# Mixing products over pairs of units, one of them on GpSimd, with transposes six units ahead

## The chip, the cores and the metric

The kernel runs on one core of a Trainium2 chip. The metric is the device time of one execution in microseconds (us); lower is better. Engines are named as the profile has them: PE is TensorE, DVE VectorE, ACT ScalarE, POOL GpSimd, SP SyncE (which only issues transfers here).

## The reference

Token mixing of an RWKV block over x of 16 batches × 2048 positions × 256 features, in float32:

```python
x_prev[:, 1:, :] = x[:, :-1, :]           # the position before; zeros at the start
...
xv = x * time_mix_v + x_prev * (1 - time_mix_v)
xr = x * time_mix_r + x_prev * (1 - time_mix_r)
...
v = xv @ value_weight
r = xr @ receptance_weight
...
out = (1 / (1 + exp(-r)) * v) @ output_weight
```

k of the reference is not used by its output. The kernel leaves it out.

## The kernel before, in words

**Units.** A batch has 2048 positions, and position p·16 + j lies in partition p, block j. A unit is four blocks of one batch, 512 positions; there are four units a batch and 64 in all. For each unit the kernel transposes x (features into partitions), mixes, projects twice (r and v), gates, projects to the output, and stores.

**The mix.** The weights are scaled by the mixing coefficient t at the start (`w_bf`), so what remains is x + c·x_prev with c = 1/t − 1 (`c_sb`). Transposed x of a batch lies in one tile `xt` with 17 slots of 128 columns: slot 1 + j holds block j, and slot 0 is block 15 moved on by one partition, a *wrap copy* (`wrap_slots`, L324), since the position before block 0 of a partition is block 15 of the partition before. x_prev of columns lo to hi is then `xt[lo:hi]` and x is `xt[lo+128:hi+128]`. So a mix is a *product*, c times `xt[lo:hi]`, one for each half `ko` of the 256 features, 128x512 each (on VectorE in `scale`, L206; on GpSimd in `scale_pool`, L216; on ScalarE in `scale_act`, L371, in the last units), and a *sum* of both halves at once, 128x1024 (`add`, L228). A *piece* is one unit's mix m: m = 0 for r, m = 1 for v.

**One iteration of the loop, unit g.** TensorE: `psum_r` (4 matmuls, L239), the transposes of a later unit (8, `ps_t`, L172), `psum_v` (4, L239), the output matmuls of unit g − 1 (8, `psum_o`, L249). ScalarE: the sigmoid `s_sb` (L390), the copy of the transposes to `xt` (L177), the copy of the output to `o_sb` (L269). VectorE: products and sums of later units, then z = s_sb · psum_v (L412), then one more sum that is *held* until behind z. GpSimd: its products, and the issue of the loads of x (L90, which also cast to bfloat16). SyncE: the stores (L259).

**What sets the order.** Each engine runs its instructions in the order in which the loop writes them; semaphores join the engines. `advance` writes the transposes of all units up to a limit: `START_T[g]` at first, then g + `LOOK`, four units ahead. It also issues the load of batch b + 2 when unit 1 of batch b is transposed. From iteration `AHEAD` (8) on, an iteration works on piece 1 of unit g + 1 and piece 0 of unit g + 2: VectorE makes the product of half 0 of both and the sum of the first; GpSimd makes the products of half 1 of both pieces of unit g + 2; the sum of piece 0 of unit g + 2 is held behind z. A manual dependency lets GpSimd start only after the last sum ahead of z.

**Buffers.** `psum_r`, `psum_v` and `psum_o` have one buffer each, `ps_t` two, `xt`, `x_bf` and `o_sb` three (a batch each), `mix` two (a batch each). So psum_v of unit g + 1 can't start before z of unit g has read its own.

Of the kernel before, what the change touches and what calls it, by code (L numbers as in the profile page):

```python
# [15 lines left out]
def kernel(  # L16
# [26 lines left out]
    KO = D // P  # L43
    J = S // P
    UJ = 4
    TU = UJ * P
    UB = J // UJ
    NU = B * UB
    LOOK = 4
    H = UJ // 2  # L50
    START_T = [1, 3, 5, 6, 7]
    AHEAD = 8
    WARM = 34
    WARM2 = 12

# [14 lines left out]
    late_copies = []  # L70
# [132 lines left out]
    def scale(piece, kos=(0, 1)):  # L203
        b, m, lo, hi = piece
        for ko in kos:
            nc.vector.tensor_scalar(  # L206
                out=mix[b][:, m, ko, lo:hi],
                in0=xt[b][:, ko, lo:hi],
                scalar1=c_sb[:, m, ko : ko + 1],
                scalar2=None,  # L210
                op0=ALU.mult,
            )

    def scale_pool(piece, after):
        b, m, lo, hi = piece
        op = nc.gpsimd.tensor_scalar(  # L216
            out=mix[b][:, m, 1, lo:hi],
            in0=xt[b][:, 1, lo:hi],
            scalar1=c_sb[:, m, 1:2],
            scalar2=1.0,  # L220
            op0=ALU.mult,
            op1=ALU.mult,
        )
        tc.add_manual_dep(op.ins, after.ins.name, SYNC, reason="one at a time")

    def add(piece):
        b, m, lo, hi = piece
        return nc.vector.tensor_tensor(  # L228
            out=mix[b][:, m, :, lo:hi],
            in0=mix[b][:, m, :, lo:hi],  # L230
            in1=xt[b][:, :, lo + P : hi + P],
            op=ALU.add,
        )

    def project(ps, g, m, lo=0, hi=TU):
        b, e = divmod(g, UB)
        for mo in range(KO):
            for ko in range(KO):
                nc.tensor.matmul(  # L239
                    out=ps[:, mo, :],  # L240
                    lhsT=w_bf[:, m, ko, mo * P : (mo + 1) * P],
                    rhs=mix[b][:, m, ko, e * TU + lo : e * TU + hi],
                    start=(ko == 0),
                    stop=(ko == KO - 1),
                )
# [15 lines left out]
    def output(g, z):  # L261
        b, e = divmod(g, UB)
        if e == 0:
            o_sb[b] = opool.tile([P, J, D], FP32, name="o_sb")
        ps = ps_o_pool.tile([P, UJ, D], FP32, name="psum_o")
        for jj in range(UJ):
            out_matmuls(ps, z, jj, jj)
        j0 = e * UJ
        nc.scalar.copy(out=o_sb[b][:, j0 : j0 + UJ, :], in_=ps)  # L269
        if b == B - 1:  # L270
            store(nc.sync, b, j0, j0 + UJ)
        elif e % 2 == 1:
            store(nc.sync, b, j0 - UJ, j0 + UJ)
# [31 lines left out]
    def tile_for(b):  # L305
        if b not in mix:
            mix[b] = mixpool.tile([P, 2, KO, J * P], BF16, name="mix")

    def pieces(g):

        b, e = divmod(g, UB)
        tile_for(b)
        return [(b, m, e * TU, (e + 1) * TU) for m in range(2)]

    def ready(g):

        b, e = divmod(g, UB)
        return tnext > (g if b == 0 else UB * b + min(e + 1, UB - 1))

    def wrap_slots():  # L320
        while late_copies:
            b = late_copies.pop()
            if b > 0:
                nc.vector.tensor_copy(  # L324
                    out=xt[b][:, :, 1:P], in_=xt[b][:, :, J * P : (J + 1) * P - 1]
                )

    tnext = 1

    def advance(limit):  # L330
        nonlocal tnext
        while tnext <= min(limit, NU - 1):
            b, e = divmod(tnext, UB)
            if e == 1 and 2 < b + 2 < B:
                load(b + 2)
            transposes(tnext)
            tnext += 1
# [23 lines left out]
    scale(pieces(1)[0])  # L361
    add(pieces(1)[0])

    z_prev = None
    elsewhere = set()
    done = 3

    def scale_act(piece, kos):
        b, m, lo, hi = piece
        for ko in kos:  # L370
            nc.scalar.activation(  # L371
                out=mix[b][:, m, ko, lo:hi],
                in_=xt[b][:, ko, lo:hi],
                func=ACT.Copy,
                scale=c_sb[:, m, ko : ko + 1],
            )
            elsewhere.add((piece, ko))

    for g in range(NU - 1):


        lead = 2 * g + (4 if g < AHEAD else 5)
        todo = [pieces(k // 2)[k % 2] for k in range(done, min(lead, 2 * NU))]
        held = todo[-1:] if lead <= 2 * NU else []
        done = lead

        ps_r = ps_r_pool.tile([P, KO, TU], FP32, name="psum_r")
        project(ps_r, g, 0)
        s_sb = zpool.tile([P, KO, TU], BF16, name="s_sb")
        nc.scalar.activation(out=s_sb, in_=ps_r, func=ACT.Sigmoid)  # L390
        advance(START_T[g] if g < len(START_T) else g + LOOK)
        if g + LOOK >= NU and g + 2 < NU:
            scale_act(pieces(g + 2)[1], (0,))
        by_pool = []
        if 0 < g < NU - 2 and ready(g + 2):
            by_pool = [p for p in pieces(g + 2) if p not in todo or p in held]
        elsewhere.update((p, 1) for p in by_pool)
        for p in todo:
            if p[0] in late_copies:
                wrap_slots()  # L400
            if g > 0:
                scale(p, [ko for ko in range(KO) if (p, ko) not in elsewhere])
        for p in todo:
            if p not in held:
                last = add(p)
        ps_v = ps_v_pool.tile([P, KO, TU], FP32, name="psum_v")
        project(ps_v, g, 1)
        if g == 0:
            scale_act(todo[0], (0, 1))
            advance(2)  # L410
        z_sb = zpool.tile([P, KO, TU], BF16, name="z_sb")
        nc.vector.tensor_tensor(out=z_sb, in0=s_sb, in1=ps_v, op=ALU.mult)  # L412
        for p in by_pool:
            if p[0] in late_copies:
                wrap_slots()
            scale_pool(p, last)
        for p in held:
            add(p)
        if z_prev is not None:
            output(g - 1, z_prev)  # L420
        z_prev = z_sb
# [31 lines left out]
```

## Time and profile before

| | before |
|---|---|
| median of 3 runs | 226.84 us (226.77 to 227.25) |
| profiled execution, its own time | 226.7 us |
| its span, first to last instruction | 224.9 us |
| mean granted clock of TensorE | 0.997 |
| HBM read, written | 34.47 MB, 33.55 MB (302 GB/s over the span) |
| VectorE products of 512 (L206), mean | 356 ns, 128 of them |
| GpSimd products of 512 (L216), mean | 694 ns, 122 of them |
| ScalarE idle ahead of the output copy (L269) | 26.6 us in all |

Durations overlap by some tens of ns on VectorE, since an instruction is counted until its last write while the next has begun; the distance from start to start is what an instruction costs there. A matmul's row lasts longer than its share of TensorE for the same reason. "Idle before" is the engine's rest ahead of an instruction, with what ended it.

### The profile page before, as it was taken

The numbers are of one execution on the slowest core, as the hardware profiler recorded it, in microseconds if no ns is written. First come the engines' busy times: TensorE is split into PE (matmuls) and PEld (weight loads), VectorE is DVE, ScalarE is ACT, GpSimd is POOL, SyncE is SP. The second block draws the span as 40 slices with busy tenths as digits, with TensorE's granted clock in tenths as the row PEclk, the third lists the DMA queues.
The fourth block names the chain that finished last, engine by engine and source line by source line (L and its number), as shares of the span: only waits on it lengthen the run. The fifth ranks groups of instructions, "written<-read, shape, count | busy, mean of one in ns | idle before, by whom it ended". The sixth has DMA issues, their size and how long they took to land.

```text
span 224.9 us, 4329 instructions
## 1 busy us (share of the span) xinstructions
PE 211.0 (94%) x1593; PEld 136.4 (61%) x1593; DVE 211.8 (94%) x354; ACT 186.5 (83%) x202; POOL 96.0 (43%) x165
## 2 busy tenths in 40 slices
PE   8799898999999999999999999999999999999891
PEld 7556564666666566666656665665666566665570
DVE  1899999999999999999999999999999999999982
ACT  2699799789888888988888898788889888888771
POOL 1714525435435452543445254344525443443420
PEclk9999999999999999999999999999999999999998
DMA  6999999696988969697896969789696974444255
GB/s 191 190 198 222 240 283 318 254 200 249 255 251 249 248 258 191 258 249 238 256 252 251 200 262 230 235 256 259 240 203 258 236 233 197 187 188 189 114 230 217
DMA packets 9341, 51.92 MB, mean 231 GB/s; under 512 B 996, under 2 KB 1896, under 8 KB 3688
## 3 DMA queue, kind: packets, MB, share of 16 engines
q0 software_dynamic: 3008, 16.39, 40.3%
q1 hardware_dynamic: 6016, 34.87, 39.1%
q10 hardware_dynamic: 296, 0.40, 0.5%
q8 instruction: 12, 0.20, 0.3%
q14 instruction: 9, 0.07, 0.1%
HBM read 34.47 MB, written 33.55 MB: 302 GB/s over the span
## 4 chain that ended last, share of the span: by engine, by line
DVE 79%; issue 6%; PE 6%; DMA 3%; POOL 1%; SPq 1%; DVEq 0%; ACT 0%; POOLq 0%
DVE mix L228 40%; DVE z_sb L412 29%; DVE mix L206 9%; DMA x_unit<-in_x_dram 3%; PE psum_v L239 2%; POOL mix L216 1%; PE psum_o L249 1%; DVE xt L324 1%; PE psum_r L239 1%; PE ps_t L172 1%; PE psum_o L172 0%; ACT xt L177 0%; PE ps_t L239 0%; DVEq L412 0%; SPq L102 0%
## 5 line engine op out<-in xcount | busy, mean ns | idle before, releaser
L216 POOL TENSOR_SCALAR mix<-xt,c_sb 128x512 bf16<-128x512 bf16 x122 | 83.4, 694 | 112.6 <-DVE mix L228 101.8
L228 DVE TENSOR_TENSOR mix<-mix,xt 128x1024 bf16<-128x1024 bf16 (+1 forms) x129 | 105.2, 817 | 0.3 <-DVE mix L206 0.2
L269 ACT COPY o_sb<-psum_o 128x1024 f32<-128x1024 f32 x62 | 62.8, 1013 | 26.6 <-PE psum_o L249 26.6
L239 PEld LDWEIGHTS <-w_bf 128*128 128x128 bf16 x520 | 49.7, 97 | 45.9 <-issue 7.2
L412 DVE TENSOR_TENSOR z_sb<-s_sb,psum_v 128x1024 bf16<-128x1024 bf16 x63 | 76.2, 1209 | 0.6 <-PE psum_v L239 0.4
L239 PE MATMUL psum_v<-mix,w_bf 128*128 128x512 bf16 (+1 forms) x256 | 65.1, 376 | 5.9 <-DVE z_sb L412 4.6
L239 PE MATMUL psum_r<-mix,w_bf 128*128 128x512 bf16 (+1 forms) x256 | 65.3, 377 | 0.2
L390 ACT ACTIVATE s_sb<-psum_r 128x1024 bf16<-128x1024 f32 x63 | 65.0, 1031 | 0.2
L249 PE MATMUL psum_o<-wo_bf,z_sb 128*128 128x256 bf16 x500 | 64.9, 273 | 0.0
L177 ACT COPY xt<-ps_t 128x1024 bf16<-128x1024 bf16 x62 | 63.1, 1021 | 0.0
L249 PEld LDWEIGHTS <-z_sb 128*128 128x128 bf16 x512 | 50.0, 98 | 19.2
L206 DVE TENSOR_SCALAR mix<-xt,c_sb 128x512 bf16<-128x512 bf16 (+1 forms) x132 | 42.6, 355 | 2.0 <-ACT xt L177 0.5
L172 PEld LDWEIGHTS <-x_bf 128*128 128x128 bf16 x496 | 32.6, 98 | 15.1 <-DMA x_bf<-in_x_dram 1.4
L172 PE MATMUL ps_t<-ident,x_bf 128*128 128x128 bf16 x496 | 37.5, 219 | 0.4 <-DMA x_bf<-in_x_dram 0.3
L90 POOL DMA_DIRECT2D x_bf<-in_x_dram x19 | 11.0, 582 | 0.3 <-issue 0.3
L128 PE MATMUL ps_t<-zeros 128*128 128x128 bf16 x46 | 4.6, 289 | 1.0 <-DVE zeros L78 1.0
L128 PEld LDWEIGHTS <-zeros 128*128 128x128 bf16 x46 | 4.3, 135 | 1.0 <-DVE zeros L78 1.0
L146 DVE COPY tm<-psum_o 128x4 f32<-128x4 f32 x1 | 0.2, 161 | 3.5 <-PE psum_o L142 3.5
L324 DVE COPY xt<-xt 128x254 bf16<-128x254 bf16 x15 | 3.2, 213 | 0.0
L111 ACT ACT_TABLE_LOAD x1 | 1.3, 1283 | 2.0 <-issue 2.0
L371 ACT ACTIVATE mix<-xt,c_sb 128x512 bf16<-128x512 bf16 x4 | 2.8, 722 | 0.0
L172 PE MATMUL psum_o<-ident_f,x_unit 128*128 128x128 f32 x8 | 1.1, 276 | 1.6 <-DMA x_unit<-in_x_dram 1.6
(45 smaller groups left out, 21.5 us busy)
## 6 DMA issues: line engine op xcount, KB each, us to landing
out_dram<-o_sb SPq DMA_DIRECT2D x30, 1024.0 KB, 5.1
x_bf<-in_x_dram POOLq DMA_DIRECT2D x14, 1024.0 KB, 11.8
x_bf<-in_x_dram POOLq DMA_DIRECT2D x4, 256.0 KB, 6.2
out_dram<-o_sb SPq DMA_DIRECT2D x2, 512.0 KB, 2.6
out_dram<-o_sb SPq DMA_DIRECT2D x3, 256.0 KB, 2.1
x_unit<-in_x_dram SPq DMA_DIRECT2D x2, 256.0 KB, 3.6
x_unit<-in_x_dram SPq DMA_DIRECT2D x1, 512.0 KB, 6.5
x_bf<-in_x_dram POOLq DMA_DIRECT2D x1, 512.0 KB, 8.9
```

The source lines that it names most:

```text
L90: nc.gpsimd.dma_start(out=x_bf[b][:, lo:hi, :], in_=rows(b)[:, lo:hi, :])
L128: nc.tensor.matmul(out=ps, lhsT=zeros, rhs=zeros, start=True, stop=True)
L172: nc.tensor.transpose(out=ps[:, ko, jj * P : (jj + 1) * P], in_=src[:, jj, ko * P : (ko + 1) * P], identity=idn,)
L177: nc.scalar.copy(out=xt[b][:, :, c0 : c0 + TU], in_=ps)
L206: nc.vector.tensor_scalar(out=mix[b][:, m, ko, lo:hi], in0=xt[b][:, ko, lo:hi], scalar1=c_sb[:, m, ko : ko + 1], scalar2=None, op0=ALU.mult,)
L216: op = nc.gpsimd.tensor_scalar(out=mix[b][:, m, 1, lo:hi], in0=xt[b][:, 1, lo:hi], scalar1=c_sb[:, m, 1:2], scalar2=1.0, op0=ALU.mult, op1 ...
L228: return nc.vector.tensor_tensor(out=mix[b][:, m, :, lo:hi], in0=mix[b][:, m, :, lo:hi], in1=xt[b][:, :, lo + P : hi + P], op=ALU.add,)
L239: nc.tensor.matmul(out=ps[:, mo, :], lhsT=w_bf[:, m, ko, mo * P : (mo + 1) * P], rhs=mix[b][:, m, ko, e * TU + lo : e * TU + hi], start=(k ...
L249: nc.tensor.matmul(out=ps[:, slot, :], lhsT=z[:, ko, jj * P : (jj + 1) * P], rhs=wo_bf[:, ko, :], start=(ko == 0), stop=(ko == KO - 1),)
L269: nc.scalar.copy(out=o_sb[b][:, j0 : j0 + UJ, :], in_=ps)
L390: nc.scalar.activation(out=s_sb, in_=ps_r, func=ACT.Sigmoid)
L412: nc.vector.tensor_tensor(out=z_sb, in0=s_sb, in1=ps_v, op=ALU.mult)
```

## The change

Three things. From unit 12 on (`PAIRS`) a product covers two neighbouring units of a batch, 1024 columns: VectorE makes half 0 and GpSimd half 1, one such product each in every iteration, in turn for m = 0 and m = 1. Sums stay by units, one ahead of z and one held behind it. GpSimd's product of an iteration is used one iteration later (`pooled[w - 1]` for `products[w]`). Before unit 12, VectorE makes both halves of piece 0 and half 0 of piece 1, GpSimd half 1 of piece 1. Transposes run six units ahead instead of four, with a longer list for the start; the point from which piece 0 is held moves from iteration 8 to 6. In the end ScalarE makes half 0 of m = 1 for two pairs, where it made it for two single units.

```diff
-    LOOK = 4
+    LOOK = 6
     H = UJ // 2
-    START_T = [1, 3, 5, 6, 7]
-    AHEAD = 8
+    START_T = [1, 3, 5, 6, 8, 9, 11, 12]
+    AHEAD = 6
+    PAIRS = 12
...
+    first = {}
+    for u in range(2, NU):
+        p0, p1 = pieces(u)
+        if u - 1 <= AHEAD:
+            sums[u - 1].append(p0)
+        else:
+            held[u - 2].append(p0)
+        (held if u - 1 < AHEAD else sums)[u - 1].append(p1)
+        first[u] = (u - 1 if u - 1 <= AHEAD else u - 2, u - 1)
+    held[0].append(pieces(1)[1])
+    for u in range(2, NU):
+        paired = u >= PAIRS
+        if paired and u % 2:
+            continue
+        for m, (b, _, lo, hi) in enumerate(pieces(u)):
+            w = first[u][m]
+            group = (b, m, lo, hi + TU if paired else hi)
+            if paired or m == 1 and w > 1:
+                products[w].append((group, (0,)))
+                pooled[w - 1].append(group)
+            else:
+                products[w].append((group, (0, 1)))
...
     for g in range(NU - 1):
-        lead = 2 * g + (4 if g < AHEAD else 5)
-        todo = [pieces(k // 2)[k % 2] for k in range(done, min(lead, 2 * NU))]
-        held = todo[-1:] if lead <= 2 * NU else []
...
         advance(START_T[g] if g < len(START_T) else g + LOOK)
-        if g + LOOK >= NU and g + 2 < NU:
-            scale_act(pieces(g + 2)[1], (0,))
-        by_pool = []
-        if 0 < g < NU - 2 and ready(g + 2):
-            by_pool = [p for p in pieces(g + 2) if p not in todo or p in held]
+        for p in products.get(g + 1, []):
+            if g + LOOK >= NU and p[0][1] == 1:
+                scale_act(p[0], (0,))
+        for p in [q for q, _ in products[g]] + pooled[g]:
...
+            if p[0] in late_copies and (g > AHEAD or p not in pooled[g]):
                 wrap_slots()
-            if g > 0:
-                scale(p, [ko for ko in range(KO) if (p, ko) not in elsewhere])
-        for p in todo:
-            if p not in held:
-                last = add(p)
+        for p, kos in products[g]:
+            if not (g - 1 + LOOK >= NU and p[1] == 1):
+                scale(p, kos)
+        for p in sums[g]:
+            last = add(p)
...
-        for p in by_pool:
+        for p in pooled[g]:
             if p[0] in late_copies:
                 wrap_slots()
             scale_pool(p, last)
-        for p in held:
+        for p in held[g]:
             add(p)
```

How the order moves on VectorE, in the iterations around unit 26, before. A sum without z's row next to it is the held one; the semaphores in brackets are those of the engine named:

```order
L228 TENSOR_TENSOR mix<-mix,xt 128x2x512 [waits Pool_49]
L206 TENSOR_SCALAR mix<-xt,c_sb 128x512
L324 COPY xt<-xt 128x2x127
L206 TENSOR_SCALAR mix<-xt,c_sb 128x512 [waits DVE_49,Activation_49]
L228 TENSOR_TENSOR mix<-mix,xt 128x2x512 [waits Pool_49]
L412 TENSOR_TENSOR z_sb<-s_sb,psum_v 128x1024 [waits PE_49,Activation_49]
```

The held sum opens the iteration, the products of two pieces follow with the wrap copy between them, and the sum ahead of z comes last. The same place on VectorE after the change, iterations 25 and 26:

```order
L229 TENSOR_TENSOR mix<-mix,xt 128x2x512 [waits DVE_49,Pool_49]
L325 COPY xt<-xt 128x2x127
L207 TENSOR_SCALAR mix<-xt,c_sb 128x1024
L229 TENSOR_TENSOR mix<-mix,xt 128x2x512 [waits DVE_49,Pool_49]
L432 TENSOR_TENSOR z_sb<-s_sb,psum_v 128x1024 [waits PE_49,Activation_49]
L229 TENSOR_TENSOR mix<-mix,xt 128x2x512
L207 TENSOR_SCALAR mix<-xt,c_sb 128x1024
L229 TENSOR_TENSOR mix<-mix,xt 128x2x512
```

One product of 1024 stands for two of 512, the wrap copy stands ahead of it, and in every second iteration the sum behind it waits for VectorE's own semaphore, in the others not. On GpSimd, over the same kind of stretch with the load of one batch, before:

```order
L134 MEMSET xt 128x2
L216 TENSOR_SCALAR mix<-xt,c_sb 128x512 [waits DVE_49,Activation_49]
L216 TENSOR_SCALAR mix<-xt,c_sb 128x512
L90 DMA x_bf<-in_x_dram 128x4096 [waits DMASW7_49,PE_49]
L216 TENSOR_SCALAR mix<-xt,c_sb 128x512 [waits DVE_49]
```

and after:

```order
L135 MEMSET xt 128x2
L217 TENSOR_SCALAR mix<-xt,c_sb 128x1024 [waits DVE_49]
L91 DMA x_bf<-in_x_dram 128x4096 [waits DMASW7_49,PE_49]
L217 TENSOR_SCALAR mix<-xt,c_sb 128x1024 [waits DVE_49,Activation_49]
L217 TENSOR_SCALAR mix<-xt,c_sb 128x1024 [waits DVE_49]
```

Where an iteration had two products of 512, it has one of 1024; the zeroing of a new `xt` and the load keep their places between them.

More of the change, by code (lines that the diff above doesn't have):

```diff
@@ L362 @@
     add(pieces(1)[0])
-    z_prev = None
-    elsewhere = set()
-    done = 3
+    sums = {g: [] for g in range(-1, NU)}
+    held = {g: [] for g in range(-1, NU)}
+    products = {g: [] for g in range(-1, NU)}
+    pooled = {g: [] for g in range(-1, NU)}
+    by_act = {g: [] for g in range(-1, NU)}
+    first = {}
[20 more added lines that the diff above has]
+                products[w].append((group, (0, 1)))
     def scale_act(piece, kos):
@@ L376, in scale_act @@
             )
-            elsewhere.add((piece, ko))
+    z_prev = None
     for g in range(NU - 1):
-        lead = 2 * g + (4 if g < AHEAD else 5)
-        todo = [pieces(k // 2)[k % 2] for k in range(done, min(lead, 2 * NU))]
-        held = todo[-1:] if lead <= 2 * NU else []
-        done = lead
         ps_r = ps_r_pool.tile([P, KO, TU], FP32, name="psum_r")
@@ L391 @@
         advance(START_T[g] if g < len(START_T) else g + LOOK)
-        if g + LOOK >= NU and g + 2 < NU:
-            scale_act(pieces(g + 2)[1], (0,))
-        by_pool = []
-        if 0 < g < NU - 2 and ready(g + 2):
-            by_pool = [p for p in pieces(g + 2) if p not in todo or p in held]
-        elsewhere.update((p, 1) for p in by_pool)
-        for p in todo:
-            if p[0] in late_copies:
-                wrap_slots()
-            if g > 0:
-                scale(p, [ko for ko in range(KO) if (p, ko) not in elsewhere])
-        for p in todo:
-            if p not in held:
-                last = add(p)
+        for p in products.get(g + 1, []):
+            if g + LOOK >= NU and p[0][1] == 1:
+                scale_act(p[0], (0,))
+        for p in [q for q, _ in products[g]] + pooled[g]:
+            assert p[0] > 0 or p[3] // TU <= tnext
+            assert p[0] == 0 or UB * p[0] + min(p[3] // TU, UB - 1) < tnext, (g, p, tnext)
+            if p[0] in late_copies and (g > AHEAD or p not in pooled[g]):
+                wrap_slots()
+        for p, kos in products[g]:
[3 more added lines that the diff above has]
+            last = add(p)
         ps_v = ps_v_pool.tile([P, KO, TU], FP32, name="psum_v")
@@ L408 @@
         if g == 0:
-            scale_act(todo[0], (0, 1))
+            scale_act(held[0][0], (0, 1))
             advance(2)
```

## The prediction

> **What bounds the kernel now.** I read the page's busy shares and the chain that ended last first, then three stretches of the run, then the instructions of one unit in order of time.
>
> ```profile
> PE 211.0 (94%) x1593; PEld 136.4 (61%) x1593; DVE 211.8 (94%) x354; ACT 186.5 (83%) x202; POOL 96.0 (43%) x165
> ...
> DVE 79%; issue 6%; PE 6%; DMA 3%; POOL 1%; SPq 1%; DVEq 0%; ACT 0%; POOLq 0%
> DVE mix L228 40%; DVE z_sb L412 29%; DVE mix L206 9%; DMA x_unit<-in_x_dram 3%; PE psum_v L239 2%; POOL mix L216 1%; PE psum_o L249 1%; DVE xt L324 1%; PE psum_r L239 1%; PE ps_t L172 1%; PE psum_o L172 0%; ACT xt L177 0%; PE ps_t L239 0%; DVEq L412 0%; SPq L102 0%
> ```
>
> VectorE and TensorE are both 94% busy, but the chain is VectorE's: the sums (L228), z (L412), the products (L206). The stretches are cut at the starts of z of units 0, 10 and 58, as the timeline has them (us, busy time and count by engine, clock, DMA share, GB/s):
>
> ```profile
> 12.23:47.40 35.17, 33.43 (x262) 21.05 (x260) 34.43 (x59) 31.37 (x35) 14.50 (x24) 1.00 0.97 251
> 47.40:204.05 156.65, 153.30 (x1154) 98.24 (x1153) 155.17 (x254) 136.48 (x145) 70.93 (x118) 1.00 0.80 233
> 204.05:224.90 20.85, 14.74 (x103) 9.46 (x101) 15.68 (x23) 12.80 (x16) 5.43 (x8) 0.97 0.50 202
> ```
>
> The middle holds 48 units in 156.65 us, 3.26 each. One of its units in order of time (start, duration):
>
> ```profile
> 102.72 1.21 DVE L412 TENSOR_TENSOR z_sb<-s_sb,psum_v 128x1024 bf16<-128x1024 bf16 x1
> ...
> 102.97 1.36 POOL L216 TENSOR_SCALAR mix<-xt,c_sb 128x512 bf16<-128x512 bf16 x2 [1.83 <-DVE mix L228]
> ...
> 103.86 1.00 DVE L228 TENSOR_TENSOR mix<-mix,xt 128x1024 bf16<-128x1024 bf16 x1
> ...
> 104.78 0.60 DVE L206 TENSOR_SCALAR mix<-xt,c_sb 128x512 bf16<-128x512 bf16 x2
> 104.85 1.04 PE L249 MATMUL psum_o<-wo_bf,z_sb 128*128 128x256 bf16 x8
> 105.31 0.68 DVE L228 TENSOR_TENSOR mix<-mix,xt 128x1024 bf16<-128x1024 bf16 x1
> 105.72 1.03 PE L239 MATMUL psum_r<-mix,w_bf 128*128 128x512 bf16 x4
> 105.91 1.21 DVE L412 TENSOR_TENSOR z_sb<-s_sb,psum_v 128x1024 bf16<-128x1024 bf16 x1
> ...
> 106.58 0.61 PE L172 MATMUL ps_t<-ident,x_bf 128*128 128x128 bf16 x8
> ...
> 107.17 1.02 PE L239 MATMUL psum_v<-mix,w_bf 128*128 128x512 bf16 x4
> ```
>
> VectorE never rests: z to z takes 3.19. The sum behind z (held, at 103.86) takes 1.00, the one ahead of z 0.68. It ends at 104.86, which is 0.53 after GpSimd's two products end at 104.33: it stands still until GpSimd is done and then runs its 0.53. So a unit is a chain: z start, 0.25 to GpSimd's start, 1.36 for its two products, 0.53 of the held sum, less 0.08 overlap, 0.53 for two products (104.78 to 105.31), 0.60 for the sum ahead of z: 3.19.
>
> One unit in four is longer by the wrap copy:
>
> ```profile
> 96.07 1.21 DVE L412 TENSOR_TENSOR z_sb<-s_sb,psum_v 128x1024 bf16<-128x1024 bf16 x1
> ...
> 98.34 0.21 DVE L324 COPY xt<-xt 128x254 bf16<-128x254 bf16 x1
> ...
> 99.53 1.22 DVE L412 TENSOR_TENSOR z_sb<-s_sb,psum_v 128x1024 bf16<-128x1024 bf16 x1
> ```
>
> 3.46 instead of 3.19, hence 3.26 on average. How near TensorE is to this shows early, where z once had to wait for it:
>
> ```profile
> 28.63 1.03 PE L239 MATMUL psum_v<-mix,w_bf 128*128 128x512 bf16 x4
> ...
> 29.76 1.22 DVE L412 TENSOR_TENSOR z_sb<-s_sb,psum_v 128x1024 bf16<-128x1024 bf16 x1 [0.38 <-PE psum_v L239]
> ...
> 31.67 1.03 PE L239 MATMUL psum_v<-mix,w_bf 128*128 128x512 bf16 x4
> ```
>
> There TensorE alone sets the pace: psum_v to psum_v in 3.04. The steady unit agrees: psum_o to psum_r 0.87, psum_r to transposes 0.86, psum_v to psum_o the same 0.86, which leaves 0.45 for eight transposes. So the most that any relief of VectorE can bring in the middle is 3.26 less 3.04, 0.22 a unit.
>
> **The change, part by part.** *Pair products on VectorE.* Two products of 512 become one of 1024. What length costs, from the start of the program:
>
> ```profile
> 7.69 0.48 DVE L206 TENSOR_SCALAR mix<-xt,c_sb 128x256 bf16<-128x256 bf16 x2
> ...
> 8.54 0.61 DVE L206 TENSOR_SCALAR mix<-xt,c_sb 128x512 bf16<-128x512 bf16 x2
> 9.19 0.69 DVE L228 TENSOR_TENSOR mix<-mix,xt 128x1024 bf16<-128x1024 bf16 x1
> ```
>
> A second product of 256 begins 0.20 after the first (0.48 less one duration, 0.28); one of 512, 0.26 after (0.61 less 0.35). So 256 elements cost 0.07, 512 more 0.14, and a pair product 0.40 instead of 0.53: 0.13 saved a unit.
>
> *Pair products on GpSimd.* Two of 512, 1.36 together, become one of 1024; call it d. No row shows that length. The rows by shape:
>
> ```profile
> L216 POOL TENSOR_SCALAR mix<-xt,c_sb 128x512 bf16<-128x512 bf16 x122 | 83.4, 694 | 112.6 <-DVE mix L228 101.8 <-DVE xt L324 6.3 <-ACT xt L177 4.5
> ...
> masks.py:199 POOL TENSOR_SCALAR_AFFINE_SELECT ident_f<-ident_f 128x128 f32<-128x128 f32 x1 | 0.3, 291 | 0.1
> ...
> L115 POOL COPY gate<-x_last 128x1 f32<-128x1 f32 x1 | 0.2, 183 | 4.4 <-DMA x_last<-in_x_dram 4.4
> ```
>
> From 128 elements (291 ns) to 512 (694 ns) an element costs 1.05 ns; from 1 (183 ns), 1.00. So d = 0.69 + 0.54 = 1.23. The upper end is 1.36, no saving at all; the lower, by the cheaper slope with room for a still larger fixed part, 1.12. I take 1.23, as the select is the nearest kind of work.
>
> The Trainium skill speaks against this: "GPSIMD Engine Reference", section 3.1, puts a tight GpSimd loop at about 1.8 cycles an element, 0.77 us for 512. By it d would be an estimated 1.46, and the unit would hardly shorten; but the whole op of 512, its start included, takes 0.69 here, so the trace already contradicts that rate.
>
> *The new unit on VectorE:* 0.25 + d + 0.53 − 0.08 + 0.40 + 0.60 = 1.70 + d = 2.93. Two things are added. In every second unit the sum ahead of z needs the pair product directly in front of it (the first two fences of the change section). There the sum behind the single product waits for VectorE's own semaphore, and the product behind the copy no longer does. Such a dependent sum begins at 9.19, 0.04 after its product's end (8.54 + 0.61), instead of 0.08 ahead of an end: 0.12 more, 0.06 a unit on average. The copy in exchange costs its bare 0.21 − 0.08 = 0.13, not 0.27: 0.03 a unit. Sum: 3.02, just under TensorE's 3.04.
>
> So TensorE becomes the pace. When VectorE runs late it has room: psum_v at 28.63, z 1.13 later, done 1.22 after that, 2.35 in all, while the next psum_v comes at 3.04; 0.69 of lateness costs nothing, and the unit with the copy needs about 0.2. I take 3.05 for the 48 units, 146.4 instead of 156.65: **10.25 gained**. With d = 1.36 VectorE stays the pace at 3.15, 151.2, and the gain is 5.45.
>
> *GpSimd's queue.* Its work goes one unit ahead; the load (its issue, 0.58, by the row below) stays between two products, and one product stands where two stood (the last two fences of the change section).
>
> ```profile
> L90 POOL DMA_DIRECT2D x_bf<-in_x_dram x19 | 11.0, 582 | 0.3 <-issue 0.3
> L134 POOL MEMSET xt<- 128x2 bf16 x15 | 1.6, 107 | 0.0
> ```
>
> GpSimd needs 0.25 + 1.23 + 0.58 + 0.11 of 3.04, so nothing queues. The transposes that a product needs are two units old, so its wait for ScalarE is over before z. The load is issued two units earlier and needed two units earlier: seven units, 21 us, against the landing below.
>
> *The ramp (z of unit 0 to 10).* Two more units of transposes are fitted in, 0.45 each on TensorE, and until unit 12 VectorE does three products of 512 and GpSimd one. GpSimd then ends 0.25 + 0.69 after z's start, before z does, so the held sum is not stopped: 1.14 + 0.60 + 3 × 0.26 + 0.60 = 3.12 a unit. Seven of these are 21.9; two copies 0.27; the copy in front of GpSimd in one unit about 0.5 (row below: two products then take VectorE 1.48, 0.9 over, with two on GpSimd; half of that with one); the unit of transition, with two products, a sum and the copy more, 4.4; unit 10, which waits for a pair product and a single one on GpSimd (1.90), 3.9; unit 1 as before 3.4. Sum 34.4.
>
> ```profile
> 9.27 2.18 POOL L90 DMA_DIRECT2D x_bf<-in_x_dram x4 [0.27 <-issue]
> ...
> 15.67 1.22 DVE L412 TENSOR_TENSOR z_sb<-s_sb,psum_v 128x1024 bf16<-128x1024 bf16 x1
> ...
> 20.62 1.64 POOL L216 TENSOR_SCALAR mix<-xt,c_sb 128x512 bf16<-128x512 bf16 x2 [2.74 <-DVE xt L324]
> ...
> 20.93 1.48 DVE L206 TENSOR_SCALAR mix<-xt,c_sb 128x512 bf16<-128x512 bf16 x2
> ...
> 23.93 0.61 PE L172 MATMUL ps_t<-ident,x_bf 128*128 128x128 bf16 x8
> ...
> x_bf<-in_x_dram POOLq DMA_DIRECT2D x1, 1024.0 KB, 13.5
> ```
>
> The first whole batch is the last of four loads that GpSimd issues from 9.27 on; it goes out at 10.8 and lands 13.5 later (the row is that of the loads issued from 10.6 to 11.2), at 24.3. Its first transposes now follow those at 23.93 at once, 0.45 behind and, with 0.4 gained by then, at about 24.0: 0.2 to 0.3 of waiting. So 34.6 against 35.17, **0.6 gained**; between −0.5 and the 3.0 that TensorE's ten units (10 × 3.04 + 4 × 0.45 = 32.2) leave.
>
> *The tail.* Six instead of four units have no transposes: 3.04 − 0.45 = 2.60 on TensorE. Of the 20.85, the four units from z of 58 to z of 62 took 11.89 (its z starts at 215.94), since psum_v waited:
>
> ```profile
> 208.50 1.02 PE L239 MATMUL psum_v<-mix,w_bf 128*128 128x512 bf16 x4 [0.43 <-DVE z_sb L412]
> ...
> 215.94 1.21 DVE L412 TENSOR_TENSOR z_sb<-s_sb,psum_v 128x1024 bf16<-128x1024 bf16 x1
> ...
> L177 ACT COPY xt<-ps_t 128x1024 bf16<-128x1024 bf16 x62 | 63.1, 1021 | 0.0
> ...
> L371 ACT ACTIVATE mix<-xt,c_sb 128x512 bf16<-128x512 bf16 x4 | 2.8, 722 | 0.0
> ```
>
> ScalarE makes two of VectorE's pair products there, at most 2 × 0.72 each; the copies of transposes that it no longer makes there (1.02 each) cover them; VectorE needs 2.53, 2.93, 2.34, 2.34 and TensorE 2.60: 10.7. **1.15 gained.** The last 8.96 stay.
>
> Sum: 12.0 off the profiled execution's 226.7 gives 214.7; the median, 226.84, is 0.14 above it: 214.8.
>
> **Rivals.** *VectorE stays the pace (0.2):* d at 1.36; 0.6 + 5.45 + 1.15 less 0.1 is 7.1, 219.7. For it: two ops of 512 show no fixed part between them (1.36 is twice 0.68). Against: 0.18 for one element.
>
> *Loads hold the old pace (0.05):* if DMA can't follow, nothing moves: 226.8. Against: share 0.80 in the middle would grow to 0.86, and 0.97 was served in the ramp.
>
> *A pair product costs GpSimd more than the two it replaces (0.05):* the held sum behind z pays every excess. Break-even is where 48 × (1.79 + d) exceeds 156.65 by ramp and tail's 1.75: d = 1.51. At 1.6 it is 162.7, **231.1**, slower. Against: an element would have to cost 1.8 ns where the rows say 1.05. By the skill's 1.8 cycles (estimated d 1.46) it would be about 224.4, still faster; that page is named above.
>
> **Numbers.** TensorE's pace, 0.7: 214.8, with ±2 from the ramp and 1.4 above from d up to 1.28. The range runs from 212.6 (ramp at TensorE's floor) to 220.0 (the first rival). Less than 0.2% either way is about what a measurement can't tell from no change. Faster 0.90, within 0.2% 0.05, slower 0.05.
>
> **What would show it.** Right: GpSimd's pair product at 1.2, the held sum near 0.9, z waiting a little for psum_v in most middle units, psum_v to psum_v 3.04, 48 units in 146. Wrong: psum_v still idle for z (first rival); psum idle for x_bf; a pair product over 1.3.

## The result, and the profile after

| | before | after |
|---|---|---|
| median | 226.81 us (226.48 to 227.25) | 214.11 us (213.77 to 214.59) |
| ratio to before | | 0.944, 95% interval 0.9416 to 0.9465 |
| profiled execution, its span | 226.7, 224.9 us | 214.59, 212.8 us |

The changed kernel is 12.7 us faster (5.6%); 214.8 was forecast. The page's busy shares and chain of what ended last, after the change:

```profile
PE 202.0 (95%) x1566; PEld 134.9 (63%) x1593; DVE 193.8 (91%) x311; ACT 186.9 (88%) x202; POOL 77.1 (36%) x104
...
PE 73%; DVE 11%; DMA 5%; ACT 4%; issue 4%; POOL 1%; ACTq 0%; DVEq 0%
PE psum_o L250 22%; PE psum_v L240 20%; PE psum_r L240 19%; PE ps_t L173 10%; DVE z_sb L432 4%; DVE mix L229 3%; DMA x_bf<-in_x_dram 3%; DVE mix L207 2%; ACT s_sb L411 2%; DMA x_last<-in_x_dram 2%; ACT xt L178 1%; ACT o_sb L270 1%; PE ps_t L240 0%; ACTq L98 0%; POOL wo_bf L118 0%
```

The chain was 79% VectorE's and is now 73% TensorE's, though TensorE's busy share rose by one point only: the chain, not the share, tells who sets the pace. The same three stretches, cut at the starts of z of units 0, 10 and 58 as before (length, busy time and count by engine, clock, DMA share, GB/s):

```profile
12.00:47.18 35.18, 33.64 (x278) 22.52 (x284) 34.29 (x67) 32.64 (x36) 9.31 (x17) 1.00 1.03 253
47.18:192.57 145.39, 143.94 (x1119) 95.57 (x1138) 139.24 (x205) 135.28 (x144) 59.29 (x69) 1.00 0.86 252
192.57:212.80 20.23, 14.73 (x100) 9.51 (x99) 13.82 (x19) 12.67 (x15) 3.35 (x3) 0.95 0.52 209
```

The ramp takes what it took (35.17), the middle 145.39 instead of 156.65, the tail 20.23 instead of 20.85; the start up to z of unit 0 is 0.23 shorter. So 11.26 of the 12.1 us of span are the middle's. Three of its units in order of time:

```profile
99.46 0.68 DVE L229 TENSOR_TENSOR mix<-mix,xt 128x1024 bf16<-128x1024 bf16 x1
...
100.06 0.48 DVE L207 TENSOR_SCALAR mix<-xt,c_sb 128x1024 bf16<-128x1024 bf16 x1
...
100.46 0.68 DVE L229 TENSOR_TENSOR mix<-mix,xt 128x1024 bf16<-128x1024 bf16 x1
...
101.37 1.22 DVE L432 TENSOR_TENSOR z_sb<-s_sb,psum_v 128x1024 bf16<-128x1024 bf16 x1 [0.23 <-PE psum_v L240]
...
102.51 0.68 DVE L229 TENSOR_TENSOR mix<-mix,xt 128x1024 bf16<-128x1024 bf16 x1
...
103.11 0.22 DVE L325 COPY xt<-xt 128x254 bf16<-128x254 bf16 x1
...
103.24 0.48 DVE L207 TENSOR_SCALAR mix<-xt,c_sb 128x1024 bf16<-128x1024 bf16 x1
...
103.83 0.69 DVE L229 TENSOR_TENSOR mix<-mix,xt 128x1024 bf16<-128x1024 bf16 x1
...
104.44 1.21 DVE L432 TENSOR_TENSOR z_sb<-s_sb,psum_v 128x1024 bf16<-128x1024 bf16 x1
104.69 1.12 POOL L217 TENSOR_SCALAR mix<-xt,c_sb 128x1024 bf16<-128x1024 bf16 x1 [2.34 <-DVE mix L229]
...
105.57 0.77 DVE L229 TENSOR_TENSOR mix<-mix,xt 128x1024 bf16<-128x1024 bf16 x1
...
106.33 1.03 PE L240 MATMUL psum_v<-mix,w_bf 128*128 128x512 bf16 x4
...
109.37 0.81 PE L240 MATMUL psum_v<-mix,w_bf 128*128 128x512 bf16 x3
```

z at 101.37 waited 0.23 for psum_v: VectorE is ahead there. The profile marks such a wait at 8 of the 48 units of the middle. The held sums (99.46, 102.51 and 105.57) take 0.68, 0.68 and 0.77 instead of 1.00. At 105.57 the sum still ends 0.53 after GpSimd (104.69 + 1.12 = 105.81; 106.34), as it did before; only GpSimd is done sooner. psum_v to psum_v is 3.04. Over a longer stretch, z of unit 22 to z of unit 54 (83.09 to 180.58), a unit takes 97.49 / 32 = 3.05; the mean over the whole middle, 145.39 / 48 = 3.03, is a little lower, because the first of its units, behind a late z of unit 10, take less. GpSimd's product by shape:

```profile
L217 POOL TENSOR_SCALAR mix<-xt,c_sb 128x1024 bf16<-128x1024 bf16 x52 | 58.0, 1116 | 91.2 <-DVE mix L229 86.6 <-ACT xt L178 4.6
```

1.12 for a pair, where 1.23 was taken and 1.12 was the lower end.

### The profile page after: what moved, and what is told of

The parts are those of the page before. It is cut to its first block, busy times and chain, and to the rows that moved or that the text cites. A ratio compares the mean times of both kernels' runs of the same rounds, so it can differ in the third digit from the quotient of the medians.

```text
span 212.8 us, 4177 instructions
## 1 busy us (share of the span) xinstructions
PE 202.0 (95%) x1566; PEld 134.9 (63%) x1593; DVE 193.8 (91%) x311; ACT 186.9 (88%) x202; POOL 77.1 (36%) x104
## 4 chain that ended last, share of the span: by engine, by line
PE 73%; DVE 11%; DMA 5%; ACT 4%; issue 4%; POOL 1%; ACTq 0%; DVEq 0%
PE psum_o L250 22%; PE psum_v L240 20%; PE psum_r L240 19%; PE ps_t L173 10%; DVE z_sb L432 4%; DVE mix L229 3%; DMA x_bf<-in_x_dram 3%; DVE mix L207 2%; ACT s_sb L411 2%; DMA x_last<-in_x_dram 2%; ACT xt L178 1%; ACT o_sb L270 1%; PE ps_t L240 0%; ACTq L98 0%; POOL wo_bf L118 0%
## 5 line engine op out<-in xcount | busy, mean ns | idle before, releaser
L217 POOL TENSOR_SCALAR mix<-xt,c_sb 128x1024 bf16<-128x1024 bf16 (+1 forms) x61 | 64.4, 1057 | 117.0 <-DVE mix L229 101.4
L229 DVE TENSOR_TENSOR mix<-mix,xt 128x1024 bf16<-128x1024 bf16 (+1 forms) x129 | 90.0, 700 | 3.0 <-DVE mix L207 0.5
L240 PEld LDWEIGHTS <-w_bf 128*128 128x128 bf16 x520 | 48.2, 98 | 35.4 <-issue 1.9
L240 PE MATMUL psum_v<-mix,w_bf 128*128 128x512 bf16 (+1 forms) x241 | 63.9, 377 | 1.7 <-DVE z_sb L432 0.6
L240 PE MATMUL psum_r<-mix,w_bf 128*128 128x512 bf16 (+1 forms) x244 | 64.0, 377 | 0.5
L178 ACT COPY xt<-ps_t 128x1024 bf16<-128x1024 bf16 x62 | 63.0, 1024 | 0.9 <-PE ps_t L173 0.9
L207 DVE TENSOR_SCALAR mix<-xt,c_sb 128x1024 bf16<-128x1024 bf16 (+2 forms) x89 | 35.5, 423 | 0.2
L399 ACT ACTIVATE mix<-xt,c_sb 128x512 bf16<-128x512 bf16 (+1 forms) x4 | 3.6, 930 | 0.0
L193 ACT CAST xt<-psum_r 128x512 bf16<-128x512 f32 x1 | 0.6, 585 | 2.5 <-PE psum_r L187 2.5
```

Source lines behind the costliest of these rows:

```text
L178: nc.scalar.copy(out=xt[b][:, :, c0 : c0 + TU], in_=ps)
L207: nc.vector.tensor_scalar(out=mix[b][:, m, ko, lo:hi], in0=xt[b][:, ko, lo:hi], scalar1=c_sb[:, m, ko : ko + 1], scalar2=None, op0=ALU.mult,)
L217: op = nc.gpsimd.tensor_scalar(out=mix[b][:, m, 1, lo:hi], in0=xt[b][:, 1, lo:hi], scalar1=c_sb[:, m, 1:2], scalar2=1.0, op0=ALU.mult, op1 ...
L229: return nc.vector.tensor_tensor(out=mix[b][:, m, :, lo:hi], in0=mix[b][:, m, :, lo:hi], in1=xt[b][:, :, lo + P : hi + P], op=ALU.add,)
L240: nc.tensor.matmul(out=ps[:, mo, :], lhsT=w_bf[:, m, ko, mo * P : (mo + 1) * P], rhs=mix[b][:, m, ko, e * TU + lo : e * TU + hi], start=(k ...
```

## The experiments

The theory: TensorE's 3.03 us a unit (the mean of the middle) is now the pace there, and what brought VectorE under it is that the held sum no longer waits for GpSimd as long. The rivals: the instruction saved on VectorE, the other split of the work alone, the look-ahead alone. In a difference below, lines are of the changed kernel unless said otherwise; a ratio is to the kernel before, run beside it.

### VectorE's pair taken apart

```diff
-                scale(p, kos)
+                b, m, lo, hi = p
+                for c in range(lo, hi, TU):
+                    scale((b, m, c, c + TU), kos)
```

> VectorE's pair product is taken apart into two products of 512 again; GpSimd keeps its pair product. Theory (TensorE is the pace in the middle, VectorE has spare time): VectorE's unit grows from 2.95 to at most 2.98, still under TensorE's 3.03, so 214.0 to 214.6 us, no change. Rival (the saving of one instruction on VectorE is what made the kernel faster): 0.13 us in each of some 50 units comes back, 220.6.

213.96 us, ratio 0.9435 (0.9412 to 0.9457): no change. The middle stretch, z of unit 10 to 58:

```profile
47.11:192.56 145.45, 143.89 (x1120) 95.46 (x1139) 143.13 (x253) 135.26 (x144) 59.28 (x69) 1.00 0.86 251
```

VectorE is 3.9 us busier there than with pairs (143.13 against 139.24) and the stretch is 0.06 longer. The pair on VectorE, by itself, is worth nothing once GpSimd has its own. Its saving on VectorE is also smaller than it looks. From the held sum to the sum ahead of z, start to start, the changed kernel took 1.00 in one unit (99.46 to 100.46) and 1.32 in the next (102.51 to 103.83), where that sum needs the pair product right in front of it. The same two places in this run (the last product row is two products):

```profile
99.39 0.68 DVE L229 TENSOR_TENSOR mix<-mix,xt 128x1024 bf16<-128x1024 bf16 x1
...
100.52 0.68 DVE L229 TENSOR_TENSOR mix<-mix,xt 128x1024 bf16<-128x1024 bf16 x1
...
102.44 0.68 DVE L229 TENSOR_TENSOR mix<-mix,xt 128x1024 bf16<-128x1024 bf16 x1
...
103.17 0.61 DVE L207 TENSOR_SCALAR mix<-xt,c_sb 128x512 bf16<-128x512 bf16 x2
103.70 0.68 DVE L229 TENSOR_TENSOR mix<-mix,xt 128x1024 bf16<-128x1024 bf16 x1
```

It takes 1.13 and 1.26. So the pair product saves 0.13 in one unit and loses 0.06 in the next.

### GpSimd's pair taken apart

```diff
-            scale_pool(p, last)
+            b, m, lo, hi = p
+            for c in range(lo, hi, TU):
+                scale_pool((b, m, c, c + TU), last)
```

> GpSimd's pair product is taken apart into two products of 512; VectorE keeps its pair product. Theory (the held sum waits until GpSimd is done, and GpSimd's time is on VectorE's path): GpSimd takes 1.36 instead of 1.12, VectorE's unit becomes 0.25 + 1.36 + 0.53 - 0.08 + 0.40 + 0.60 = 3.06, with the drain and the wrap copy 3.18, above TensorE's 3.03: 48 units in 153 us, 221 to 222. Rival (GpSimd's work is hidden, being one unit ahead): 214.1.

221.46 us, ratio 0.9775 (0.9743 to 0.9808), as the theory had it. GpSimd's two products, the held sum, and the middle stretch:

```profile
99.16 1.36 POOL L217 TENSOR_SCALAR mix<-xt,c_sb 128x512 bf16<-128x512 bf16 x2 [1.58 <-DVE mix L229]
...
100.12 0.94 DVE L229 TENSOR_TENSOR mix<-mix,xt 128x1024 bf16<-128x1024 bf16 x1
```
```profile
48.33:200.62 152.29, 148.73 (x1124) 97.32 (x1142) 149.44 (x206) 136.17 (x144) 70.85 (x117) 1.00 0.80 240
```

The drain in the expectation is the later start of a sum that needs the product in front of it. The held sum ends at 101.06, 0.54 after GpSimd (100.52). GpSimd's work is used a unit later and no one waits for its data; still, 0.24 us more of it makes the middle 6.9 longer, 0.14 a unit. An engine that is idle for more than half of the stretch (70.85 of 152.29 busy) is on the path by standing in VectorE's way.

The Trainium skill, "SBUF — State Buffer", section "Who interferes with whom", has the rule behind this: a VectorE instruction with two inputs in SBUF and a GpSimd instruction that reads SBUF want the same port, and the one that has it holds it to its end. The trace agrees, with the 0.53 and 0.54 above.

### The held sum left out

```diff
         for p in held[g]:
-            add(p)
+            if UB * p[0] + p[2] // TU < PAIRS:
+                add(p)
```

> Leaves out the sum behind z from unit 12 on (the r mix then lacks x), 0.6 to 0.7 us of VectorE's work a unit, and with it the wait for GpSimd. Theory (TensorE is the pace): the middle stays at 3.03 a unit, only the catching up at its start goes, 213.3 to 214.1. Rival (VectorE is still what sets the pace, TensorE just follows): 0.6 us off each of 48 units until ScalarE's 2.75 stops it, about 201.

213.4 us, ratio 0.9415 (0.9395 to 0.9436). The middle stretch, and the wait that took the sum's place:

```profile
46.83:192.14 145.31, 143.88 (x1119) 95.42 (x1138) 110.28 (x158) 135.20 (x144) 59.74 (x70) 1.00 0.87 252
```
```profile
DVE z_sb L432 <- PE psum_v L240: 30.6, 44, 0.8
```

29 us of VectorE's work are gone (110.28 against 139.24), and z waits 30.6 us for psum_v instead, 44 times over the run. The middle is 0.08 shorter, and z of unit 22 to z of unit 54 takes 97.49 us, as in the changed kernel and in the run with VectorE's pair taken apart. So TensorE's pace it is, and no more relief of VectorE can help there.

### No pairs at all, twice

```diff
-    PAIRS = 12
+    PAIRS = NU
...
             if g + LOOK >= NU and p[0][1] == 1:
+                if p[0][0] in late_copies:
+                    wrap_slots()
                 scale_act(p[0], (0,))
```

> No pairs at all: all units keep the scheme of the ramp (three products of 512 on VectorE, one of 512 on GpSimd), look-ahead and order of sums as changed; the wrap copy of the last batch stands one line earlier. Theory: VectorE's unit is 3.12 as in the ramp's last units, with the wrap copy 3.16, above TensorE's 3.03: 48 units in 151.5 us, 220.2; so half of the gain is the other split between VectorE and GpSimd, which no longer stops the held sum, and half the pairs. Rival (pairs are all of it): back to about 226.8. Rival (the look-ahead is all of it): 214.1.

227.19 us, ratio 1.0033 (1.0015 to 1.0051): 7 us over what the theory had. Units took the 3.12 that was expected, but every eighth took 4.61:

```profile
99.97 0.36 DVE L325 COPY xt<-xt 128x254 bf16<-128x254 bf16 x2 [1.14 <-ACT xt L178]
```
```profile
DVE xt L325 <- ACT xt L178: 7.1, 6, 1.4
```

`wrap_slots` makes the wrap copies of all batches whose last block has been transposed. Six units ahead, the next batch's block is transposed in the very iteration that first needs this batch's copy, so two copies are written, the newer batch's first, and that one waits for ScalarE to have copied the transposes. With pairs GpSimd's product asks for the copy a unit sooner, when only one is pending. I had missed this. The next run has `PAIRS = NU` too, without the second part of the difference above, and the copy at that place:

```diff
+        if g > AHEAD and (g + 3) % UB == 0:
+            wrap_slots()
```

> No pairs, as before, but the wrap copy of a batch stands where the changed kernel has it, one unit sooner than in the run without pairs before this one. There VectorE stood 1.14 us for ScalarE's copy of a later batch's transposes and made two wrap copies, once in eight units (4.61 instead of 3.12), since the copy came due in the iteration that transposes the next batch. Theory (that place alone cost it): all units 3.12, with the copy 3.26, 48 units in 151.5 us, 219.5 to 220.5. Rival (the scheme without pairs is no better than the old one for another reason): 226 to 227.

219.44 us, ratio 0.9677 (0.9661 to 0.9693). The middle stretch:

```profile
45.94:197.49 151.55, 149.38 (x1125) 97.81 (x1145) 151.55 (x302) 136.19 (x144) 38.94 (x69) 1.00 0.85 243
```

151.55, to the tenth the 151.5 that was expected, with VectorE never idle. So of the middle's 11.26 us, 5.1 come without any pairs and 6.2 with them. The 5.1 are of two kinds: a unit takes 3.12 instead of 3.19, since GpSimd's single product ends under z (48 times, 3.4 us), and the wrap copy adds 0.14 instead of 0.27, since it stands at another place (12 times, 1.6 us). This run has the look-ahead as well; its own share in the 5.1 isn't told apart.

### Half of the output projection left out

```diff
-            out_matmuls(ps, z, jj, jj)
+            for ko in range(KO if g < PAIRS else 1):
+                nc.tensor.matmul(
...
```

> Leaves out half of the output projection (its second half of the features) from unit 12 on, 0.44 us of TensorE's work a unit. Theory (TensorE is the pace, VectorE close behind it): VectorE's 2.95 takes over from 3.03 in the middle, 4 us less there and up to 1 in the tail, 209 to 211. Rival (VectorE has a lot of room, as its 0.6 us less in the run without the held sum might suggest): the full 0.44 a unit until ScalarE's 2.75, 200 to 202. Rival (TensorE isn't the pace): 214.

208.89 us, ratio 0.9222 (0.9197 to 0.9247). The chain by engine, and the middle stretch:

```profile
DVE 64%; issue 15%; ACT 8%; DMA 5%; PE 3%; POOL 1%; DVEq 0%; ACTq 0%
```
```profile
46.41:187.31 140.90, 131.61 (x942) 79.60 (x959) 138.05 (x205) 135.68 (x145) 59.44 (x69) 1.00 0.91 259
```

With an estimated 21 us less for TensorE in the middle (48 × 0.44, half of the 0.87 from psum_o to psum_r), only 4.5 are gained: VectorE takes over at 140.90 / 48 = 2.94 a unit. By these means over the middle the two engines lie 0.09 apart.

### The look-ahead alone, in the kernel before

```diff
-    LOOK = 4
+    LOOK = 6
...
-    START_T = [1, 3, 5, 6, 7]
+    START_T = [1, 3, 5, 6, 8, 9, 11, 12]
...
-        if g + LOOK >= NU and g + 2 < NU:
+        if g + 4 >= NU and g + 2 < NU:
```

> The kernel before with the look-ahead and the starting list of the change alone. Theory (VectorE's 3.26 is the pace and the look-ahead doesn't touch it; TensorE's earlier transposes fall into its spare time; VectorE is the pace in the tail too): 226.5 to 227.2, no change. Rival (the look-ahead brings part of the gain, in the tail): 225.5.

229.33 us, ratio 1.011 (1.0095 to 1.0125): 1.1% slower, which neither side had. It is the same trap as above:

```profile
100.34 0.36 DVE L324 COPY xt<-xt 128x254 bf16<-128x254 bf16 x2 [0.54 <-ACT xt L177]
```
```profile
DVE xt L324 <- ACT xt L177: 3.2, 6, 0.5
```

Six such waits, 3.2 us in all. Before, no wrap copy waited for ScalarE. In the old order the look-ahead costs by itself. It is harmless where the copy is asked for a unit sooner, by GpSimd's pair products as in the changed kernel or directly as in the second run without pairs. What it brings once the copy is out of the way was not run.

### Five units ahead, and a start of the pairs two units sooner

Beside these three runs the changed kernel was run again, as their base:

> The changed kernel unaltered, as the base for the three runs beside it on the same chip: 213.7 to 214.5.

213.82 us (213.58 to 214.47), ratio 0.9436 (0.942 to 0.9452). With `LOOK = 5`:

> Transposes five units ahead instead of six, the starting list unaltered (from iteration 8 on one unit less). Pairs still find their transposes done. Theory (in the middle TensorE has the same work a unit, only the tail loses one unit without transposes, 0.45 of TensorE's time, and ScalarE takes over one pair product less there): 214.2 to 214.8. Rival (the sixth unit is needed so that products don't wait for transposes): 217 or more, with VectorE or GpSimd waiting for ScalarE's copies in the middle.

214.43 us, ratio 0.9463 (0.9443 to 0.9483): within the theory's numbers, and with the intervals overlapping not told apart from six. The rival's sign did come: GpSimd waited for ScalarE's copies 16 times, 42.1 us in all, against 4 times and 11.9 us in the changed kernel. But its products are used a unit later, and the middle takes 145.81 against 145.39. Then ScalarE's products of the tail, one of 512 in each iteration:

```diff
-        for p in products.get(g + 1, []):
-            if g + LOOK >= NU and p[0][1] == 1:
-                scale_act(p[0], (0,))
+        if g + LOOK >= NU and g + 2 < NU:
+            scale_act(pieces(g + 2)[1], (0,))
```

> Only ScalarE's products of the tail in four halves. Theory: z no longer waits 0.36 for the sigmoid there, 0.2 to 0.4 less than the changed kernel beside it, 213.7 to 213.9. Rival (the tail is given by TensorE and the last stores): equal.

213.88 us, ratio 0.9434 (0.9421 to 0.9448): equal. The wait that it aims at is real in the changed kernel, and z of unit 59 has none of that size here (first row after the change, second this run):

```profile
195.36 1.22 DVE L432 TENSOR_TENSOR z_sb<-s_sb,psum_v 128x1024 bf16<-128x1024 bf16 x1 [0.36 <-ACT s_sb L411]
```
```profile
194.23 1.22 DVE L431 TENSOR_TENSOR z_sb<-s_sb,psum_v 128x1024 bf16<-128x1024 bf16 x1
```

But what it saves is less than executions differ. Last, the same with `PAIRS = 10`, first and again beside the changed kernel:

> Two changes to the changed kernel: pairs from unit 10 on, and in the tail ScalarE makes a product of 512 in each of four iterations instead of one of 1024 in two, so that the sigmoid is not late (z waited 0.36 and 0.25 for it there). Theory: 0.3 to 0.6 in the tail, 0.2 to 0.3 in the ramp, where two units take VectorE 2.95 instead of 3.12; 213.2 to 213.7. Rival (TensorE's work up to the end sets the time whatever VectorE does in the ramp): only the tail, 213.6 to 214.1.

213.18 us, ratio 0.9401 (0.9385 to 0.9416).

> Pairs from unit 10 and ScalarE's products of the tail in four halves, once more beside the changed kernel. Theory (0.3 in the tail, up to 0.6 in the ramp): 0.4 to 0.9 less than the changed kernel beside it, 213.2 to 213.7. Rival (the 213.18 of the first time was the chip): equal within 0.3.

212.95 us, ratio 0.9397 (0.9384 to 0.941), 0.87 less than the changed kernel beside it, and the best version found. From z of unit 1 to 10 it takes 30.61, the changed kernel 31.01:

```profile
15.64:46.25 30.61, 30.04 (x251) 20.24 (x253) 30.23 (x55) 28.87 (x32) 10.17 (x17) 1.00 1.03 254
```
```profile
16.17:47.18 31.01, 30.56 (x253) 20.66 (x257) 30.73 (x59) 29.39 (x33) 9.31 (x17) 1.00 1.02 262
```

That is 0.4 of the 0.87; the tail's 0.26 from unit 58 to 62 was in the run before as well and brought nothing measurable there. In both profiled executions of this version the last store lands 2.9 us after its issue, in both of the changed kernel 3.5; that is 0.6 more, and nothing here shows that the edit is its cause. The rest stays open.

## Why the prediction was right, point by point

The mechanism held, and its main step was measured by itself. That the sum came so near (12.0 forecast, 12.1 in the spans, 12.7 in the medians) is in part luck: the middle brought 1.0 more than forecast and the start 0.2, ramp and tail together 1.1 less.

- *TensorE becomes the pace, at 3.04 to 3.05 a unit.* Right: 3.05 over units 22 to 54, 145.39 for 48 units against 146.4. The 1.0 over is that z of unit 10 comes late against TensorE and the units behind it catch up. The run without the held sum shows the pace directly. One sign that was named did not come: z waits visibly for psum_v in 8 of the 48 units, not in most, since VectorE is only about 0.1 us a unit faster than TensorE.
- *d, GpSimd's pair product.* 1.12, at the lower end; 1.23 was too long, since the nearest rows (a select, one-element copies) did not have this instruction's fixed part. It mattered little, because TensorE ended the gain; the sum's first rival needed 1.36.
- *The held sum pays every excess of GpSimd.* Right, and measured by itself: 6.9 us for 0.24 a unit. VectorE's own 2.94 and 0.24 more make 3.18; the run with GpSimd's pair taken apart has 152.29 / 48 = 3.17.
- *The pair on VectorE saves 0.13 a unit.* Right in every second unit (1.00 against 1.13). In the others the dependent sum takes more than that back (1.32 against 1.26), so the pair saves VectorE about 0.035 a unit on average. The sum had both terms, with 0.06 a unit for the second, and so 0.07 in all; what it was worth was nothing, since TensorE was the pace.
- *A dependent sum costs 0.12 more.* It is 0.19: the sum at 103.83 begins 0.11 after its product's end, and the one at 100.46, which doesn't need the product in front of it, 0.08 ahead of that product's end. VectorE's own unit came to 2.94 (half of the output left out), not 3.02, mostly because d was 1.12 and not 1.23.
- *The wrap copy gets cheaper.* Right in size (103.11 to 103.24), with no dependent product behind it. What was not seen is the condition: it must be asked for before the next batch's transposes are. Two runs show what happens otherwise.
- *The ramp gains 0.6.* Zero in the profiled executions. From unit 1 to 10 it gains 0.72 (31.73 to 31.01 in the stretch from z to z), as worked out; the first unit lost the same, because the first loads landed later there and TensorE stood waiting:

```profile
14.58 0.62 PE L173 MATMUL ps_t<-ident,x_bf 128*128 128x128 bf16 x8 [0.89 <-DMA x_bf<-in_x_dram]
```

  The order of instructions up to there is the same in both kernels and in all runs, and z of unit 0 to unit 1 took 4.17 in this execution but 3.42 with five units ahead (first row to second, below) and up to 4.73 in the other runs. So this is the spread of executions and not the change:

```profile
11.56 1.21 DVE L432 TENSOR_TENSOR z_sb<-s_sb,psum_v 128x1024 bf16<-128x1024 bf16 x1
...
14.98 1.22 DVE L432 TENSOR_TENSOR z_sb<-s_sb,psum_v 128x1024 bf16<-128x1024 bf16 x1
```

- *The tail gains 1.15.* From unit 58 to 62 it does (11.89 to 10.70, as worked out), though with ScalarE late where the sum had it covered. 0.6 is given back at the very end, where the last store lands 3.5 us after its issue instead of 2.9 (first row before, second after); it took 2.9 again in the last experiment, but 3.5 in the changed kernel's second profile and 2.8 with VectorE's pair taken apart, whose last instructions are the same. So the change is not shown to be its cause, and what decides it stays open:

```profile
out_dram<-o_sb ACTq DMA_DIRECT2D x1, 256.0 KB, 2.9
```
```profile
out_dram<-o_sb ACTq DMA_DIRECT2D x1, 256.0 KB, 3.5
```

- *Loads hold the old pace.* They don't: the middle's DMA share is 0.86, exactly the figure worked out.
- *The range.* Two of its figures don't follow from the sum: 3.0 instead of 0.6 in the ramp gives 212.4, not 212.6, and d up to 1.28 adds 48 × 3.07 less 146.4, 1.0, not 1.4. Nothing else hangs on them.

## What to carry to other kernels

An engine that is busy a third or half of the time can set the pace through what it blocks: follow the instruction that takes longer than its own kind, and see whose end it follows. Before costing an edit on the bound engine, work out where the next engine's floor lies; here 3.26 could fall to 3.05 and no further, and the pair on VectorE was not needed for it. A saving on one instruction can be lost on the next: look at what now stands right behind its own input. When work is moved earlier, look at what else its trigger sweeps along: a helper that handles "everything pending" may start to wait for something that nobody needs yet.

## What the runs showed of the hardware that was not expected

A GpSimd product of 1024 takes 1.12 us and one of 512 0.69: between the two 0.82 ns an element, which leaves a fixed 0.27, more than the other GpSimd rows had suggested. The Trainium skill's "GPSIMD Engine Reference" says in section 4.1 that one-input work runs there at roughly line rate; by its 1.2 GHz that is an estimated 0.83 ns, which the trace bears out. The 1.8 cycles of its section 3.1 are no figure for this instruction.

A sum that needs the VectorE product directly in front of it starts 0.19 us later than one that doesn't, by the rows of the changed kernel (103.24 to 103.83 against 100.06 to 100.46). One unrelated instruction between them hides that: with VectorE's pair taken apart, the second of two products stands between, and the sum (103.70) begins 0.08 ahead of that product's end (103.17 + 0.61).
